# A combination in twelve pieces, single copies of q, and two weight splits two token pairs earlier

## The chip, the cores and the metric

The kernel is one program on one core of a Trainium2 chip. The metric is the device time of one execution in microseconds (us). The engines are TensorE (PE; PEld is its weight load), VectorE (DVE), ScalarE (ACT) and GpSimd (POOL); SyncE (SP) issues most DMAs. Each engine takes its instructions in order.

## The reference

The reference is one decoder layer on 2048 tokens of 1024 columns, in float32. Two mixers read the same normed input; the second is attention over three branches, whose results are weighted with the softmax denominators.

```python
h = rms_norm(x, g_mix[l]); z = h @ w_in[l]
u, gb, gc, q, k, v = jnp.split(z, splits, axis=-1)
y_conv = gb * short_conv(gc * u, conv_w[l])            # causal, depthwise, width 3
q = rms_norm(q, g_q[l]) * HEAD_DIM ** -0.5; k = rms_norm(k, g_k[l])      # 8 heads of 64
y_attn = dilated_mixture(q, k, v)         # (window, dilation) = (128,1), (512,4), (2048,16)
mix = concat(rms_norm(y_conv, g_conv_out[l]), rms_norm(y_attn, g_attn_out[l]))
x = x + mix @ w_out[l]
h = rms_norm(x, g_ffn[l])
x = x + (silu(h @ w_gate[l]) * (h @ w_up[l])) @ w_down[l]
```

## The kernel before

Large products are made of fp16 pairs: a value is a high part and a `low` rest, and three products of such parts replace one in float32. A tile framework orders the instructions of each engine: by the order in which the code writes them, by when a tile's buffer is free, and by `issue_after`, which keeps what stands in its block behind a given instruction.

The stages, in the order of the span:

- **Norms and the first quarter of the conv mixer** (0 to 105 us). `conv_steps` makes channel block `j` in four chunks `c` of 512 tokens. In the first quarter the squares of a chunk (`c2`) are summed over channels by four small TensorE matmuls into a `tr` tile (`squares`, L354, L358); the squares of chunk c − 1 are summed within chunk c, the last ones in `last_squares` (L1211).
- **The q/k/v projection** (105 to 363). Sixteen units `project(g, c)`: group `g` of two heads, token block `c`. The matmuls (L1205) fill banks that ScalarE evacuates (`f`, L1221); then q and k are normed and split (`qkhl`, L1250), stored to DRAM (`d_qk`, L1254) and read back transposed into `qT`, `ka`, `kb` (L199). Beside the units run jobs from a list: `operands` (the next group's weights), `spill_conv` (conv weights through `d_wc`, L1277) and `spill_out` (w_out's raw halves, L1287, split into `t` and stored to `d_wo`, L1306). Raw tiles of w_out and the work tiles of `spill_conv` share the buffers `t4`.
- **Attention** (384 to 712, filled with steps of the conv's other three quarters and of the first part of the output product). 160 units: group, head and branch in the order b = 1, 2, 0, with 8, 4 and 8 units a head. A unit makes scores on TensorE (L1467), exponentials on ScalarE (L1472), the causal band by selects on GpSimd (L1480), a cast on ScalarE (L1483) and `low` on VectorE (L1484). Three units later TensorE makes its output (L1494), and VectorE copies it into `u` (L1499, L1502). Branch 2 reads a copy of q in another token order, `regroup` (L1375, the copies L1380): four copies on VectorE for each head, written at `count` 9 of a group (its second head) and 33 (the next group's first head). `combine` (L1411) adds the three branches' results (L1417, L1418) on GpSimd, takes the reciprocal of the weights' sum with four small VectorE operations (L1420 to L1423), multiplies (L1427) and stores to `d_y` (L1430). It works on eight of sixteen token tiles at once, as four entries of `todo`, due four units on; for the last head it works on four tiles at once on VectorE.
- **The output product** (730 to 905). Eight pairs of token tiles `p` in `out_b`: norm, product, residual, norm for SwiGLU, `hl` stored to `d_h`. Behind two of the pairs stands `left` (L729), the split of a weight's first block for SwiGLU (`w_gate`, then `w_up`): loads `wq`, scaling on ScalarE (L742), sums on GpSimd, rests on VectorE (L723).
- **SwiGLU** (905 to 1720) reads `d_h` transposed; its first products (L812) are evacuated at L863. **The down product** (1720 to 2119) ends the kernel.

Of the kernel before, what the change touches and what calls it, by code (L numbers as in the profile page):

```python
# [18 lines left out]
P = 128  # L19
# [3 lines left out]
NT = S // P  # L23
# [7 lines left out]
class Builder:  # L31
# [170 lines left out]
    def run(self):  # L202
        tc, nc, A = self.tc, self.nc, self.A
        with ExitStack() as ctx:
# [16 lines left out]
            self.dmin = cp.tile([P, 18], F32, name="dmin")  # L221
# [384 lines left out]
    def out_b(self):  # L606
        tc, nc, A = self.tc, self.nc, self.A
        with ExitStack() as c:
# [77 lines left out]
            for p in range(8):  # L686
# [11 lines left out]
                if p in (3, 5):  # L698

                    with tc.issue_after(self.dve.ins), tc.issue_after(self.act.ins), tc.issue_after(self.sp.ins):  # L700
                        self.Wn.append(self.left(A[("w_gate", "w_up")[len(self.Wn)]][0], 0))
# [309 lines left out]
class Fast(Builder):  # L1011
# [22 lines left out]
    def in_and_conv(self):  # L1034
# [5 lines left out]
        with ExitStack() as c:  # L1040
# [42 lines left out]
            n = -1  # L1083
            for step in self.conv_steps(0, W, before):
# [3 lines left out]
                if n == 6:  # L1088
                    norms.close()
                    with tc.issue_after(self.act.ins):  # L1090
                        nc.scalar.preload_act_table_set("natural_log_exp_and_others")
                    self.ring = e(tc.tile_pool(name="ring", bufs=8, side="right"))
# [13 lines left out]
            for n in range(16):  # L1106
# [3 lines left out]
                with ExitStack() as behind:  # L1110
# [13 lines left out]
                    if n == 14:  # L1124
                        self.regroup(self.st0, 0)
# [57 lines left out]
    def project(self, g, c, W):  # L1183
# [27 lines left out]
        def last_squares():  # L1211
            if (g, c) == (0, 0):
                self.squares(3, self.last, self.pstr.tile([P, 4], F32, name="tr"), False)
# [66 lines left out]
    def spill_out(self, half, m):  # L1280
# [4 lines left out]
        for q in range(2):  # L1285
            raw = self.tmp.tile([P, 4, 256], F32, name="t4")
# [22 lines left out]
    def conv_steps(self, j, W, before=None):  # L1309
# [4 lines left out]
        for c in range(4):  # L1314
# [19 lines left out]
            if late is not None:  # L1334
                self.squares(c - 1, late, self.few() if j else self.pstr.tile([P, 4], F32, name="tr"), j > 0)
# [19 lines left out]
            s2 = self.sq[c] if j == 1 else self.cs.tile([P, 512], F32, name="c2", bufs=2)  # L1355
# [5 lines left out]
            late = s2 if j in (0, 3) else None  # L1361
        self.last = late
# [12 lines left out]
    def regroup(self, st, h):  # L1375
# [3 lines left out]
        for n in range(4):  # L1379
            self.nc.vector.tensor_copy(t[:, :, 32 * n:32 * n + 32],  # L1380
                                       st["qT"][:, h, 512 * n:512 * (n + 1)].rearrange("p (a r) -> p r a", r=NT))

# [15 lines left out]
    def attn_steps(self, g, st, nx):  # L1398
# [7 lines left out]
        for h, b in [(h, b) for h in range(2) for b in (1, 2, 0)]:  # L1406
# [4 lines left out]
            def combine(c, n, h=h, last=last):  # L1411

                ts = slice(c, c + n)
                bm = self.at.tile([P, NT], F32, name="bm", bufs=2)[:, 0:n]
                X = [r[:, ts] for r in (U[h, 0], R[h, 1], R[h, 2])]
                e = nc.vector if last else nc.gpsimd
                e.tensor_tensor(X[1], X[1], X[2], op=ALU.add)  # L1417
                e.tensor_tensor(X[0], X[0], X[1], op=ALU.add)  # L1418
                d = 2 * (2 * g + h) + c // n
                nc.vector.tensor_reduce(self.dmin[:, d:d + 1], X[0][:, :, HD], axis=AX.X, op=ALU.min)  # L1420
                nc.vector.tensor_scalar_max(bm, X[0][:, :, HD], 2.0 ** -7)
                nc.vector.reciprocal(bm, bm)
# [472 lines left out]
```

## Time and profile before

| | us |
|---|---|
| median of 3 runs | 2126.46 |
| lowest and highest run | 2121.56, 2128.05 |
| the profiled execution | 2120.59 |
| its span | 2118.8 |
| TensorE busy in it | 2019.1 |
| VectorE, ScalarE, GpSimd busy | 1348.2, 1008.9, 775.3 |

A row of the profile gives the line of the code, the engine, the operation and the tiles (out<-in), a count, and either busy time and mean duration, or a start and a duration; in brackets stands the idle time of the engine ahead of it and what ended that. SPq is SyncE's queue. The granted clock is TensorE's, 1.00 being full speed. Stages are read from the rows' times; one runs into the next.

### The profile page before, as it was taken

The numbers are of one execution on the slowest core, as the hardware profiler recorded it, in microseconds if no ns is written. First come the engines' busy times: TensorE is split into PE (matmuls) and PEld (weight loads), VectorE is DVE, ScalarE is ACT, GpSimd is POOL, SyncE is SP. The second block draws the span as 40 slices with busy tenths as digits, with TensorE's granted clock in tenths as the row PEclk, the third lists the DMA queues.
The fourth block names the chain that finished last, engine by engine and source line by source line (L and its number), as shares of the span: only waits on it lengthen the run. The fifth ranks groups of instructions, "written<-read, shape, count | busy, mean of one in ns | idle before, by whom it ended". The sixth has DMA issues, their size and how long they took to land.

```text
span 2118.8 us, 34786 instructions
## 1 busy us (share of the span) xinstructions
PE 2019.1 (95%) x13368; PEld 1123.8 (53%) x13368; DVE 1348.2 (64%) x2515; ACT 1008.9 (48%) x1780; POOL 775.3 (37%) x809
## 2 busy tenths in 40 slices
PE   4999989999899899989999999999999999999998
PEld 2499989666566544434444444444444444444443
DVE  7455443567777866886767676676768575555453
ACT  7446655666566566552434333334333344343341
POOL 0026535457666521222212212231222245555463
PEclk9999999999999999999999999999999999999999
DMA  9558984356857567995333223322322762431442
GB/s 242 151 136 213 247 205 121 106 151 133 180 139 218 152 191 230 260 296 160 110 109 105 82 92 105 115 87 93 110 100 90 273 238 60 142 117 55 149 140 81
DMA packets 460272, 317.02 MB, mean 150 GB/s; under 512 B 255681, under 2 KB 413377, under 8 KB 457921
## 3 DMA queue, kind: packets, MB, share of 16 engines
q1 hardware_dynamic: 442416, 291.56, 48.4%
q10 hardware_dynamic: 17680, 23.16, 3.0%
q8 instruction: 106, 1.74, 0.3%
q14 instruction: 70, 0.57, 0.1%
HBM read 157.96 MB, written 116.85 MB: 130 GB/s over the span
## 4 chain that ended last, share of the span: by engine, by line
PE 65%; DVE 10%; DMA 8%; ACT 6%; issue 4%; POOL 4%; SPq 3%; DVEq 0%; ACTq 0%; POOLq 0%
PE ps L812 34%; PE ps L945 15%; PE mm L191 3%; PE mm L192 3%; PE mm L193 3%; POOL sm L1480 2%; PE cvx L1205 2%; PE s L1467 1%; PE av L1494 1%; SPq L199 1%; PE mm L1205 1%; DVE vm_a L96 1%; DMA nx_x<-in_x_dram 1%; DVE et L1484 1%; DMA b<-d_h 1%
## 5 line engine op out<-in xcount | busy, mean ns | idle before, releaser
L812 PEld LDWEIGHTS <-w 128*128 128x128 f16 x3696 | 362.2, 98 | 450.7 <-issue 15.3
L812 PE MATMUL ps<-b,w 128*128 128x512 f16 x2112 | 465.4, 381 | 9.9 <-ACT s L863 5.4
L945 PE MATMUL ps<-b,w 128*128 128x512 f16 x1848 | 399.7, 379 | 2.4 <-DVE x L953 1.2
L812 PE MATMUL ps<-hb,w 128*128 128x512 f16 x1584 | 347.1, 379 | 0.8 <-ACT s L863 0.8
L945 PEld LDWEIGHTS <-w 128*128 128x128 f16 x1848 | 180.8, 98 | 221.1 <-issue 3.5
L1205 PEld LDWEIGHTS <-b 128*128 128x128 f16 x3072 | 255.0, 98 | 9.8 <-issue 9.3
L705 POOL TENSOR_TENSOR t<-wq 128x512 f32<-128x512 f32 (+1 forms) x46 | 59.7, 1297 | 407.2 <-issue 230.6
L1480 POOL TENSOR_SCALAR_AFFINE_SELECT sm<-sm 128x256 f32<-128x256 f32 (+2 forms) x288 | 142.2, 517 | 119.9 <-ACT sm L1472 105.8
L818 DVE TENSOR_TENSOR s<-ps,s 128x512 f32<-128x512 f32 x220 | 150.1, 683 | 38.3 <-PE ps L812 37.8
L1484 DVE TENSOR_TENSOR et<-sm,et 128x512 f16<-128x512 f32 (+1 forms) x160 | 129.3, 816 | 67.1 <-ACT et L1483 65.4
L952 POOL TENSOR_TENSOR x<-x,s 128x512 f32<-128x512 f32 x72 | 103.1, 1432 | 171.3 <-DVE s L966 132.2
L1205 PE MATMUL cvx<-w,b 128*128 128x192 f16 x1776 | 151.2, 246 | 0.7 <-ACT f L1221 0.6
L1483 ACT CAST et<-sm 128x512 f16<-128x512 f32 (+1 forms) x160 | 93.8, 589 | 93.3 <-POOL sm L1480 92.3
L953 DVE SCALAR_TENSOR_TENSOR x<-ps,a_u,x 128x512 f32<-128x512 f32 x96 | 71.8, 749 | 101.1 <-PE ps L945 74.3
L1472 ACT ACTIVATE sm<-s,bound,kap 128x512 f32<-128x512 f32 (+1 forms) x160 | 118.6, 747 | 25.9 <-PE s L1467 21.7
L192 PE MATMUL mm<-b,wq 128*128 128x512 f16 x320 | 122.7, 384 | 0.0
L193 PE MATMUL mm<-b,wq 128*128 128x512 f16 x320 | 122.7, 383 | 0.0
L191 PE MATMUL mm<-b,wq 128*128 128x512 f16 x320 | 122.6, 383 | 0.0
L1205 PE MATMUL mm<-w,b 128*128 128x192 f16 x1296 | 113.1, 248 | 8.2 <-ACT f L1221 8.2
L722 ACT CAST w<-t 128x512 f16<-128x512 f32 x88 | 53.7, 616 | 128.6 <-PE ps L812 86.6
L1494 PE MATMUL av<-v,et 128*128 128x65 f16 x1800 | 86.2, 195 | 27.6 <-DVE et L1484 20.4
L96 DVE TENSOR_REDUCE vm_a<-wq 128x1 f32<-128x2048 f32 (+2 forms) x32 | 77.4, 2417 | 41.0 <-DMA wq<-in_w_up_dram 19.8
(289 smaller groups left out, 3242.1 us busy)
## 6 DMA issues: line engine op xcount, KB each, us to landing
d_a<-a ACTq DMA_DIRECT2D x88, 256.0 KB, 2.0
d_wd<-w SPq DMA_DIRECT2D x77, 256.0 KB, 2.0
wq<-d_a SPq DMA_DIRECT2D x64, 256.0 KB, 4.1
b<-d_wd SPq DMA_DIRECT2D x14, 1024.0 KB, 6.6
wq<-in_w_in_dram SPq DMA_DIRECT2D x24, 512.0 KB, 6.5
d_qk<-qkhl SPq DMA_DIRECT2D x16, 768.0 KB, 4.8
d_h<-hl SPq DMA_DIRECT2D x24, 512.0 KB, 3.1
wq<-in_w_gate_dram SPq DMA_DIRECT2D x22, 512.0 KB, 4.7
```

The costliest lines, as they stand in the source:

```text
L191: self.pe = mm(ps, lhsT=lh(k), rhs=rh(k), start=k == ks[0], stop=False)
L192: mm(ps, lhsT=lh(k), rhs=rl(k), start=False, stop=False)
L193: mm(ps, lhsT=ll(k), rhs=rh(k), start=False, stop=k == ks[-1])
L812: nc.tensor.matmul(ps[self.BANK[n]], lhsT=w[:, x, k], rhs=b[:, y, k], start=first and k == 0 and q == 0, stop=k == 3 and q == 2, skip_grou ...
L818: nc.vector.tensor_tensor(t, x, y, op=ALU.add)
L945: nc.tensor.matmul(ps[self.BANK[n]], lhsT=L[n][:, x, f], rhs=B[n][:, f, y], start=first and f == 0 and q == 0, stop=f == n_f - 1 and q == ...
L952: nc.gpsimd.tensor_tensor(o, o, s_, op=ALU.add)
L1205: self.pe = nc.tensor.matmul(ps[:, 192 * t:192 * (t + 1)], lhsT=lh(x, k), rhs=w[:, y, k], start=start and t + k + q == 0, stop=stop and k ...
L1472: nc.scalar.activation(e, sp[:, 0:o], AF.Exp, scale=self.kap, bias=self.bound)
L1480: sel = nc.gpsimd.affine_select(m, m, pattern=pattern, compare_op=ALU.is_ge, fill=0.0, base=0, channel_multiplier=-sg)
L1484: nc.vector.tensor_tensor(et[:, 1], e, et[:, 0], op=ALU.subtract)
L1494: self.pe_av = nc.tensor.matmul(ps[:, us.index(u)], lhsT=p_, rhs=v_, start=n_ == 0, stop=n_ == len(ops) - 1)
```

## The change

Five edits. The four squares of the conv's first quarter are all summed in `last_squares`, in the first unit of the projection, with four `c2` buffers. w_out's raw tiles have a pool of their own (`raws`, two buffers). `regroup` is a generator, and in attention one copy is written at each of the counts 9, 11, 13, 15 and 32, 34, 36, 38, behind that unit's `low`; the block ahead of attention stays whole. `combine` works on four token tiles at once, in twelve steps: add, add with the small operations, and so on four times, then four multiplications with their stores; they are due 2 to 13 units on, one a unit, and `u` has four buffers. The `left` splits stand behind pairs p = 1 and 3 rather than 3 and 5.

```diff
-                if p in (3, 5):
+                if p in (1, 3):
...
+                    self.raws = e(tc.tile_pool(name="raws", bufs=2, side="right"))
...
             if (g, c) == (0, 0):
-                self.squares(3, self.last, self.pstr.tile([P, 4], F32, name="tr"), False)
+                for k in range(4):
+                    self.squares(k, self.sums[k], self.pstr.tile([P, 4], F32, name="tr"), False)
...
-            raw = self.tmp.tile([P, 4, 256], F32, name="t4")
+            raw = self.raws.tile([P, 4, 256], F32, name="raw")
...
-            if late is not None:
-                self.squares(c - 1, late, self.few() if j else self.pstr.tile([P, 4], F32, name="tr"), j > 0)
+            if late is not None and j:
+                self.squares(c - 1, late, self.few(), True)
...
-            def combine(c, n, h=h, last=last):
+            def combine(chunks, e, h=h, last=last):
...
+                for c in chunks:
+                    ts = slice(c, c + 4)
+                    e.tensor_tensor(X[1][:, ts], X[1][:, ts], X[2][:, ts], op=ALU.add)
                     yield
+                    e.tensor_tensor(X[0][:, ts], X[0][:, ts], X[1][:, ts], op=ALU.add)
+                    d, w = 4 * (2 * g + h) + c // 4, X[0][:, ts, HD]
+                    nc.vector.tensor_reduce(self.dmin[:, d:d + 1], w, axis=AX.X, op=ALU.min)
+                    nc.vector.tensor_scalar_max(bm[:, ts], w, 2.0 ** -7)
+                    nc.vector.reciprocal(bm[:, ts], bm[:, ts])
+                    nc.vector.tensor_scalar_mul(bm[:, ts], bm[:, ts], uv)
+                    yield
+                for c in chunks:
+                    ts = slice(c, c + 4)
+                    x = X[0][:, ts, 0:HD]
+                    y = self.y7[:, ts] if last else x
+                    e.tensor_tensor(y, x, bm[:, ts].unsqueeze(2).broadcast_to([P, 4, HD]), op=ALU.mult)
+                    if not last:
+                        i = (2 * g + h) * HD
+                        nc.sync.dma_start(self.d_y.rearrange("(t p) c -> p t c", p=P)[:, ts, i:i + HD], y)
+                    yield
-            Ub = U[h, b] = self.up.tile([P, NT, HD + 1], F32, name="u", bufs=3)
+            Ub = U[h, b] = self.up.tile([P, NT, HD + 1], F32, name="u", bufs=4)
...
-                            for i, step_ in enumerate(c for m in (0, 8) for c in [combine(m, 8)] * 2):
-                                self.todo.append((self.n + 4 + i, lambda step_=step_: next(step_, None)))
+                            steps = combine((0, 4, 8, 12), nc.gpsimd)
+                            for i in range(12):
+                                self.todo.append((self.n + 2 + i, lambda: next(steps)))
...
                     if count == 9:
-                        self.regroup(st, 1)
-                    if count == 33 and g < 3:
-                        self.regroup(nx, 0)
+                        order = self.regroup(st, 1)
+                    if count == 32 and g < 3:
+                        order = self.regroup(nx, 0)
+                    if count in (9, 11, 13, 15, 32, 34, 36, 38):
+                        with self.tc.issue_after(low.ins):
+                            next(order, None)
```

The first place is SyncE's queue in the projection, from the conv weights' stores to the next `d_qk` store. Before, the raws of w_out's first half (`t_1559`, `t_1561`) stand there:

```order
55 L1287 DMA t_1559<-in_w_out_dram 128x4x256
56 L1232 DMA d_v_61<-vs_977 128x4x130
57 L199 DMA_TRANSPOSE ka<-d_qk_132 128x2x512
58 L1277 DMA d_wc_129<-t_1555 128x2048
59 L1135 DMA wq<-in_w_in_dram 128x8x128
60 L1287 DMA t_1561<-in_w_out_dram 128x4x256
61 L1135 DMA wq<-in_w_in_dram 128x8x128 x2
62 L199 DMA_TRANSPOSE kb<-d_qk_132 128x2x512
63 L1254 DMA d_qk_132<-qkhl 128x4x768
```

Now these two raws stand at row 38, ahead of the first of these transposes, and the raws here are those of the next half:

```order
57 L199 DMA_TRANSPOSE ka<-d_qk_132 128x2x512
58 L1280 DMA d_wc_129<-t_1558 128x2048
59 L1137 DMA wq<-in_w_in_dram 128x8x128 x3
60 L199 DMA_TRANSPOSE kb<-d_qk_132 128x2x512
61 L1309 DMA d_wo_81<-t_1815 128x4x256
62 L1309 DMA d_wo_81<-t_1821 128x4x256
63 L1309 DMA d_wo_81<-t_1815 128x4x256
64 L1290 DMA raw<-in_w_out_dram 128x4x256
65 L1235 DMA d_v_61<-vs_963 128x4x130
66 L1309 DMA d_wo_81<-t_1821 128x4x256
67 L1235 DMA d_v_61<-vs_963 128x4x130
68 L1290 DMA raw<-in_w_out_dram 128x4x256
```

The loads from w_out have moved ahead of the group, and the stores of their split (`d_wo`) stand ahead of the next `d_qk`.

The second place is VectorE's queue in attention, at the copies of q for the second head of the second group. Before, the four copies (L1380) stand nearly together, between two of the combination's small operations:

```order
440 L1420 TENSOR_REDUCE dmin<-u 128x1
441 L1421 TENSOR_SCALAR bm<-u 128x8
442 L1380 COPY q_6900<-qT 128x16x32 x3
443 L1422 RECIPROCAL bm<-bm 128x8
444 L1380 COPY q_6900<-qT 128x16x32
445 L1502 COPY u<-av 128x260
446 L1423 TENSOR_SCALAR bm<-bm,uv 128x8
447 L1484 TENSOR_TENSOR et<-sm,et 128x512 x2
```

After, for the same head, the copies (L1385) stand apart; here the second and the third, with `low` (now L1494), copies of outputs (L1512) and conv operations (L1349, L1350) between them:

```order
521 L1385 COPY q_6920<-qT 128x16x32
522 L1430 TENSOR_SCALAR bm<-bm,uv 128x4
523 L1349 SCALAR_TENSOR_TENSOR cg<-cu,convw,cg 128x512
524 L1494 TENSOR_TENSOR et<-sm,et 128x384
525 L1512 COPY u<-av 128x260
526 L1408 TENSOR_SCALAR uv<-uq 128x1
527 L1350 SCALAR_TENSOR_TENSOR cg<-cu,convw,cg 128x512
528 L1494 TENSOR_TENSOR et<-sm,et 128x512
529 L1385 COPY q_6920<-qT 128x16x32
530 L1512 COPY u<-av 128x260
```

Two units lie from one copy to the next.

The third place is GpSimd's queue at a head's combination: the adds (L1417, L1418), the multiplications (L1427) and the selects (L1480) before:

```order
122 L1417 TENSOR_TENSOR r_5617<-r_5617,r_5759 128x520
123 L1480 AFFINE_SELECT sm<-sm 128x2x128 x2
124 L1418 TENSOR_TENSOR u<-u,r_5617 128x520
125 L1480 AFFINE_SELECT sm<-sm 128x512
126 L1417 TENSOR_TENSOR r_5617<-r_5617,r_5759 128x520
127 L1480 AFFINE_SELECT sm<-sm 128x512
128 L1418 TENSOR_TENSOR u<-u,r_5617 128x520
129 L1427 TENSOR_TENSOR u<-u,bm 128x8x64
130 L1480 AFFINE_SELECT sm<-sm 128x512 x2
131 L1427 TENSOR_TENSOR u<-u,bm 128x8x64
```

And the second half of the adds and the first multiplications now (L1423, L1425, L1436, selects L1490):

```order
129 L1425 TENSOR_TENSOR u<-u,r_5619 128x260
130 L1490 AFFINE_SELECT sm<-sm 128x512
131 L1423 TENSOR_TENSOR r_5619<-r_5619,r_5763 128x260
132 L1490 AFFINE_SELECT sm<-sm 128x512
133 L1425 TENSOR_TENSOR u<-u,r_5619 128x260
134 L1490 AFFINE_SELECT sm<-sm 128x2x128
135 L1490 AFFINE_SELECT sm<-sm 128x128
136 L1436 TENSOR_TENSOR u<-u,bm 128x4x64
137 L1490 AFFINE_SELECT sm<-sm 128x2x128 x2
138 L1436 TENSOR_TENSOR u<-u,bm 128x4x64
```

Between two pieces of half as many columns stands one unit's selects.

More of the change, by code (lines that the diff above doesn't have):

```diff
@@ L220, in run @@
             self.eps = cp.tile([P, 3], F32, name="eps")
-            self.dmin = cp.tile([P, 18], F32, name="dmin")
+            self.dmin = cp.tile([P, 32], F32, name="dmin")
             self.low = cp.tile([P, 1], F32, name="low")
@@ L1082, in before @@
                     norm(14, 2)
-            n = -1
+            n, self.sums = -1, []
             for step in self.conv_steps(0, W, before):
@@ L1124, in in_and_conv @@
                     if n == 14:
-                        self.regroup(self.st0, 0)
+                        for _ in self.regroup(self.st0, 0):
+                            pass
                 self.project(g, 3 - i if g == 3 else i, Wg)
@@ L1354, in conv_steps @@
                                     apply_absolute_value=True)
-            s2 = self.sq[c] if j == 1 else self.cs.tile([P, 512], F32, name="c2", bufs=2)
+            s2 = self.sq[c] if j == 1 else self.cs.tile([P, 512], F32, name="c2", bufs=2 if j else 4)
             nc.scalar.activation(s2, y, AF.Square)
@@ L1361, in conv_steps @@
             late = s2 if j in (0, 3) else None
+            if j == 0:
+                self.sums.append(s2)
         self.last = late
@@ L1409, in attn_steps @@
             last = g == 3 and h == 1
-            def combine(c, n, h=h, last=last):
[L1413 to L1422, printed above, removed]
-                nc.vector.tensor_scalar_mul(bm, bm, uv)
-                if not last:
-                    yield
-                y = self.y7[:, ts] if last else X[0][:, :, 0:HD]
-                e.tensor_tensor(y, X[0][:, :, 0:HD], bm.unsqueeze(2).broadcast_to([P, n, HD]), op=ALU.mult)
-                if not last:
-                    i = (2 * g + h) * HD
-                    nc.sync.dma_start(self.d_y.rearrange("(t p) c -> p t c", p=P)[:, ts, i:i + HD], y)
@@ L1431, in attn_steps @@
-            Ub = U[h, b] = self.up.tile([P, NT, HD + 1], F32, name="u", bufs=3)
+            def combine(chunks, e, h=h, last=last):
+                bm = self.at.tile([P, NT], F32, name="bm", bufs=2)
+                X = U[h, 0], R[h, 1], R[h, 2]
+                for c in chunks:
+                    ts = slice(c, c + 4)
+                    e.tensor_tensor(X[1][:, ts], X[1][:, ts], X[2][:, ts], op=ALU.add)
+                    yield
+                    e.tensor_tensor(X[0][:, ts], X[0][:, ts], X[1][:, ts], op=ALU.add)
[13 more added lines that the diff above has]
+                        nc.sync.dma_start(self.d_y.rearrange("(t p) c -> p t c", p=P)[:, ts, i:i + HD], y)
+                    yield
@@ L1483, in attn_steps @@
                     nc.scalar.copy(et[:, 0], e)
-                    nc.vector.tensor_tensor(et[:, 1], e, et[:, 0], op=ALU.subtract)
+                    low = nc.vector.tensor_tensor(et[:, 1], e, et[:, 0], op=ALU.subtract)
                     def output(us=us, pr=pr, et=et, at=at, av=av, b=b, h=h, Vb=Vb, Ub=Ub, step=step, done=pr[-1] == us[-1],
@@ L1503, in output @@
                         if last and b == 0:
-                            for _ in combine(us[0], 4):
+                            for _ in combine(us[0:1], nc.vector):
                                 pass
```

## Prediction

> **What bounds the kernel now.** I read the page first, then TensorE's waits, then tables by stage, and last the rows around each wait that the change touches. The page's first part:
>
> ```profile
> PE 2019.1 (95%) x13368; PEld 1123.8 (53%) x13368; DVE 1348.2 (64%) x2515; ACT 1008.9 (48%) x1780; POOL 775.3 (37%) x809
> ```
>
> TensorE is the bound: of the span of 2118.8 us it idles for 2118.8 − 2019.1 = 99.7 us. A change that leaves its matmuls as they are can win only from these, and from the time in which the clock is held low after them. What TensorE waited for, largest first (total, times, longest):
>
> ```profile
> PE cvx L191 <- DMA b<-ka: 24.8, 1, 24.8
> PE av L1494 <- DVE et L1484: 20.4, 17, 4.2
> PE av L1494 <- DVE u L1502: 5.1, 3, 2.0
> PE av L1494 <- DVE u L1499: 1.2, 1, 1.2
> ```
>
> The 24.8 us are the kernel's first load; the change leaves it. The other three are the attention stage, where most of the change works. Stretches of the span (start and end, width, busy time of PE, PEld, DVE, ACT, POOL with counts, then granted clock, DMA share, GB/s):
>
> ```profile
> 400.00:700.00 300.00, 276.52 (x3178) 186.27 (x3177) 216.77 (x371) 194.06 (x324) 188.75 (x301) 0.98 0.63 157
> ```
>
> ```profile
> 284.00:300.00 16.00, 7.84 (x75) 7.40 (x73) 5.45 (x6) 16.00 (x31) 4.45 (x4) 0.79 0.54 147
> 531.00:540.00 9.00, 5.57 (x40) 3.21 (x41) 6.87 (x11) 2.37 (x4) 4.78 (x7) 0.62 0.69 184
> 905.00:915.00 10.00, 4.57 (x14) 1.67 (x13) 9.96 (x11) 10.00 (x22) 6.33 (x4) 0.66 1.10 325
> ```
>
> In attention TensorE is busy 276.5 of 300 us, so 23.5 us lie idle; VectorE is busy 72% and GpSimd 63%. The three short stretches hold one long wait each (shown below), and the clock is 0.62 to 0.79 there: a wait costs more than itself. After 531, 9.0 × 0.38 = 3.4 us of full clock are missing, part of them inside the wait itself; I charge 2 us to each wait of this size.
>
> **The change part by part.**
>
> *The projection.* The rows of the longest wait, on SyncE's queue, GpSimd, ScalarE and TensorE:
>
> ```profile
> 264.25 8.09 SPq L199 DMA_TRANSPOSE ka<-d_qk  x1
> 277.18 1.90 POOL L1243 TENSOR_TENSOR row<-f,qkr_y 128x1024 f32<-128x1024 f32 x1 [11.58 <-DVE vm_t L101]
> 282.12 0.71 ACT L1250 CAST qkhl<-row 128x256 f16<-128x256 f32 x2 [12.55 <-DMA d_qk<-qkhl]
> 291.96 0.56 ACT L1221 ACTIVATE f<-mm,uq 128x384 f32<-128x384 f32 x1
> 292.57 2.72 PE L1205 MATMUL mm<-w,b 128*128 128x192 f16 x16 [8.16 <-ACT f L1221]
> ```
>
> TensorE has no free bank until ScalarE evacuates at 291.96. ScalarE stood behind its cast at 282.12, held by the store d_qk, which SyncE issues in order behind the raw loads of w_out; those waited for buffers that the split of the conv weights still held. The new pool removes that: SyncE's order after has the raws of the first half ahead of everything in question, those of the second behind the d_wo stores that free them. With a split of w_out one unit ahead of the operands' split, an evacuation stands between the two on ScalarE. Gone is 8.2 and about 1.8 of clock; but the transposes at 264.25 stay and are queued ahead of the same store. Ends: −10 and −4; I take **−8**. Four squares more after conv piece 3 instead of one each:
>
> ```profile
> 78.14 1.05 PE L358 MATMUL tr<-ones,c 128*128 128x1 f32 x8 [1.73 <-ACT c L1356]
> 87.15 0.39 PE L192 MATMUL cvx<-b,wq 128*128 128x512 f16 x1 [2.35 <-DMA b<-kb]
> ```
>
> The work is the same, two groups of eight being moved from ahead of the load wait that ends at 87.15 (where shorter matmul work only lengthens the wait) to behind it, about 1 us each with the edges: **+1.9** (0, if they find another gap, to +2.4). The two more c2 buffers and wider dmin are memory only.
>
> *q's copies.* TensorE's waits beside the last five of the six blocks of four copies that ran in attention:
>
> ```profile
> 449.90 0.22 PE L1494 MATMUL av<-v,et 128*128 128x65 f16 x2 [2.02 <-DVE u L1502]
> 450.64 0.48 PE L1494 MATMUL av<-v,et 128*128 128x65 f16 x10 [0.51 <-DVE et L1484]
> 491.38 0.22 PE L1494 MATMUL av<-v,et 128*128 128x65 f16 x2 [1.53 <-DVE u L1502]
> 492.71 0.48 PE L1494 MATMUL av<-v,et 128*128 128x65 f16 x10 [1.10 <-DVE et L1484]
> 534.43 0.73 PE L1494 MATMUL av<-v,et 128*128 128x65 f16 x10 [4.20 <-DVE et L1484]
> 579.69 0.73 PE L1494 MATMUL av<-v,et 128*128 128x65 f16 x10 [3.63 <-DVE et L1484]
> 624.39 0.22 PE L1494 MATMUL av<-v,et 128*128 128x65 f16 x2 [1.53 <-DVE u L1502]
> 625.72 0.48 PE L1494 MATMUL av<-v,et 128*128 128x65 f16 x10 [1.11 <-DVE et L1484]
> ```
>
> ```profile
> 529.12 3.21 DVE L1380 COPY q<-qT 128x512 f16<-128x512 f16 x3
> L1380 DVE COPY q<-qT 128x512 f16<-128x512 f16 x32 | 23.9, 798 | 0.0
> ```
>
> Their sum is 15.6; ten output matmuls last 0.73 instead of 0.48 after the two longest, where the clock is low: with 2 us for each, 19.6. Four copies (4 × 0.80 = 3.2 us) stood in VectorE's queue ahead of the `low` subtraction that the output waits for. Now one copy follows a `low`, every second unit. A unit lasts 2.05 us (160 from 384 to 712), an output comes three units after its scores, so a delay of 0.8 us is below that slack. But 28 copies stand in attention rather than 24 (one block that had run before it is spread as well), and VectorE, at 72%, must absorb them: 28 × 0.2 = 5.6 stays by my choice. **−14.0**, ends −19.6 and −8. The copies' readers come later than they: the first two of a block are done before unit 40, the others before unit 44. No new wait there.
>
> *The combination.* Its present rows on GpSimd, one there with half as many columns, the selects (column after the bar: busy us, mean ns, idle before), and its small operations on VectorE:
>
> ```profile
> L1418 POOL TENSOR_TENSOR u<-u,r 128x520 f32<-128x520 f32 x14 | 21.6, 1543 | 0.4
> L1417 POOL TENSOR_TENSOR r<-r,r 128x520 f32<-128x520 f32 x14 | 20.8, 1487 | 0.0
> L1427 POOL TENSOR_TENSOR u<-u,bm 128x512 f32<-128x512 f32 x14 | 19.6, 1397 | 10.0 <-DVE bm L1423 7.5 <-DVE cvr_t L52 2.0 <-DVE ssa L362 0.5
> L1253 POOL TENSOR_TENSOR qkhl<-row,qkhl 128x256 f16<-128x256 f32 x32 | 21.8, 703 | 12.3 <-ACT qkhl L1251 12.3
> L1480 POOL TENSOR_SCALAR_AFFINE_SELECT sm<-sm 128x256 f32<-128x256 f32 (+2 forms) x288 | 142.2, 517 | 119.9 <-ACT sm L1472 105.8 <-DVE et L1484 6.9 <-DVE u L1502 3.8
> ```
>
> ```profile
> L1423 DVE TENSOR_SCALAR bm<-bm,uv 128x8 f32<-128x8 f32 (+1 forms) x18 | 7.6, 420 | 0.2
> L1421 DVE TENSOR_SCALAR bm<-u 128x8 f32<-128x8 f32 (+1 forms) x18 | 6.0, 336 | 0.0
> L1422 DVE RECIPROCAL bm<-bm 128x8 f32<-128x8 f32 (+1 forms) x18 | 3.4, 187 | 0.1
> L1420 DVE TENSOR_REDUCE dmin<-u 128x1 f32<-128x8 f32 (+1 forms) x18 | 2.8, 156 | 4.9 <-POOL u L1418 4.9
> ```
>
> GpSimd: 42 operations (62.0 us) become 84. At 256 columns a similar one took 0.70, half of 1.54 is 0.77: 84 × 0.77 = 64.7 us, the same total, but a select behind one waits 0.8 us instead of 3 (two adds together). Attention's waits in the three rows above are 20.4 + 5.1 + 1.2 = 26.7 us; without the copies' 15.6 and the end's 1.2 + 2.3 (below) 7.6 are left. They fall beside these adds and would go. Against it stand 14 more sets of four small VectorE operations, each of (7.6 + 6.0 + 3.4 + 2.8)/18 = 1.10 us: +15.4 us, of which the 28% of free VectorE time covers most; a quarter, 3.9, reaches TensorE. **−3.7**, ends −7.6 and +4. The Trainium skill's page "GPSIMD Engine Reference" (section "Specifications") says that GpSimd's SBUF interfaces are shared with VectorE and contend with VectorE instructions that have two SBUF inputs, as `low` has; the same bytes would then slow it as much in pieces as whole, which makes this term 0 and the sum −22.1. The trace goes further: copies with one input took 3.21/3 = 1.07 us beside GpSimd's work, 0.80 on average. Fourteen more d_y stores go through SyncE, half as large; v and r, queued behind them, are wanted eight units later, so they cost nothing while that lead of 16 us lasts.
>
> *The end of attention.* The last waits, 1.2 and this one, were beside the last combination on GpSimd:
>
> ```profile
> 709.65 0.73 PE L1494 MATMUL av<-v,et 128*128 128x65 f16 x10 [2.33 <-DVE et L1484]
> ```
>
> With clock that is 5 us; the pieces now end later against the tail, so some stays: **−1** (−5 to +3).
>
> *The weight splits of SwiGLU.*
>
> ```profile
> 910.44 1.86 PE L812 MATMUL ps<-b,w 128*128 128x512 f16 x4 [5.43 <-ACT s L863]
> 943.57 2.86 PE L812 MATMUL ps<-b,w 128*128 128x512 f16 x9 [2.71 <-DMA b<-d_h]
> 730.00:830.00 100.00, 97.40 (x460) 44.14 (x460) 69.65 (x168) 61.06 (x120) 21.10 (x26) 0.98 0.73 221
> 830.00:905.00 75.00, 69.30 (x319) 30.89 (x317) 63.42 (x118) 45.08 (x73) 15.36 (x9) 1.00 0.86 252
> ```
>
> The split of the second weight falls at 830 to 905, where VectorE is busy 85%. Two pairs earlier, VectorE has 30 us free in 100; a split costs it some 10 us (63.42 against 0.70 × 75 = 52.2). So it crowds pairs 2 to 4 and frees 5 to 8: the start at 910.44 loses the scaling ahead of its evacuation and should give up 3 of its 5.4, while the later wait at 943.57 rests on transposes through DRAM and grows by about 2 when TensorE comes sooner. **−1** (−6 to +3).
>
> Sum against the profiled execution's 2120.59 us: −8 + 1.9 − 14.0 − 3.7 − 1 − 1 = −25.8. That execution stands 5.9 us below the runs' median of 2126.46, and the difference is carried over: 2126.46 − 25.8 = **2100.7**.
>
> **The rivals.** *A, half comes back.* The projection's wait stays, because the 8.09 us transpose and not the raws holds the store (+8), and the copies each cost their unit 0.35 us instead of 0.2 (+4): −13.8, 2112.7. For it: the transposes' length; against it: the raws are out of that queue in the new order.
>
> *B, the transfers take it back.* All that is won ahead of 905 returns at SwiGLU's start, if that waits on DMA: the share is 1.10 at 905. Then −25.8 becomes about −2: 2124. Against it: only 2.7 us were waited there, and the weights' loads move out of that stretch.
>
> *C, slower: GpSimd's pieces cost by the instruction.* The selects take 142.2/160 = 0.89 us of a unit's 2.05. If a piece of half the columns takes over the other 1.16, the twelve units that hold one overrun. At 1.3: 12 × (1.3 + 0.89 − 2.05) = 1.7 us a head and over seven heads 12, plus the low clock, 2 each, 14, plus 7 × 1.2 as the small operations of VectorE wait behind them: 34 against −25.8, so 2135. Row L1253 speaks against it, since 0.70 us is far below 1.16.
>
> *D, it doesn't do what it says.* The scheduler could pull the pieces or copies together again; the order after does not show it.
>
> **How the numbers follow.** Forecast (−15 to −40) 0.66; A 0.18; B 0.09; C 0.07; D has no time of its own and lies within B. From A almost all is faster by over 0.3% (6.4 us, about what a measurement of this kernel can tell from no change). Range: 2086, where all the better ends but a few come together (−10, 0, −19.6, −7.6, −2, −1: −40), to 2120, which takes in A whole and leaves out B and C. Faster 0.84, same 0.09, slower 0.07.
>
> **What would show it.** Right: no TensorE wait over 2 us between 250 and 300; no [4.20] or [3.63] in attention, and its idle time in that stage from 23.5 to under 10 us; GpSimd's 128x260 adds near 0.77 us; the wait on L863 under 3 us. Wrong: a d_qk store still late behind the transposes (A); the wait of L812 on b<-d_h growing past 10 us (B); 128x260 adds over 1.1 us, and selects as releasers (C).

## The result and the profile after

| | kernel before, us | changed kernel, us | ratio, 95% interval |
|---|---|---|---|
| first comparison, medians | 2127.26 | 2099.47 | 0.9874 (0.9852 to 0.9896) |
| second, beside later experiments | 2121.67 | 2099.82 | 0.9903 (0.9888 to 0.9918) |

The change is worth 27.8 us by the first and 21.8 us by the second; 2100.7 and a gain of 25.8 had been forecast. The changed kernel's median hardly differs; the other one's does. By stage, the profiled executions side with the second. A stage runs here to the end of the last matmul of its kind, or to the start of the next kind (projection L1205, now L1207; outputs of attention L1494, now L1504; SwiGLU L812; down L945):

| stage, us | before | after | after, second profile |
|---|---|---|---|
| up to the projection | 105.0 | 104.0 | 103.3 |
| projection | 265.6 | 260.7 | 259.7 |
| attention | 364.1 | 345.0 | 344.9 |
| output product | 162.5 | 167.5 | 167.0 |
| SwiGLU | 812.9 | 813.9 | 813.1 |
| down product, to the last matmul | 402.0 | 402.3 | 402.4 |

The sum is 2112.1 before, 2093.4 and 2090.4 after: 19 to 22 us. Attention won 19, the first two stages 6 to 8, and the output product gave 4.5 to 5 back. TensorE's row of the page after:

```profile
PE 2017.7 (96%) x13368; PEld 1121.5 (53%) x13368; DVE 1345.2 (64%) x2571; ACT 1009.2 (48%) x1780; POOL 793.9 (38%) x851
```

It idles 2099.9 − 2017.7 = 82.2 us of its span, 17.5 less than before. Its waits, the kernel's first loads left out:

```profile
PE av L1504 <- DVE et L1494: 8.5, 19, 1.2
...
PE ps L812 <- DVE s L818: 4.1, 2, 3.5
PE ps L812 <- DMA b<-d_h: 4.0, 1, 4.0
PE mm L191 <- DVE qT L660: 3.8, 1, 3.8
PE ps L191 <- ACT b L585: 3.0, 1, 3.0
PE av L1504 <- DVE u L1512: 2.5, 2, 1.6
PE ps L812 <- ACT s L863: 2.4, 1, 2.4
...
PE cvx L1207 <- ACT f L1224: 1.9, 2, 1.3
```

The wait on the projection's f is 1.3 at the longest instead of 8.2. In attention no wait on VectorE's `low` (L1494) is over 1.2, where 4.2 and 3.6 stood. What is late next is all behind attention: the output product's waits of 3.0 and 3.8 and SwiGLU's start. The same stretch of attention as before (width, then busy times, clock, DMA share):

```profile
400.00:700.00 300.00, 285.98 (x3295) 192.20 (x3293) 226.74 (x487) 200.84 (x337) 215.64 (x359) 1.00 0.67 167
```

Idle time there is 14.0 us instead of 23.5, and the clock is 1.00 instead of 0.98. The prediction had named under 10 us as a sign of being right; that was missed. The 26.9 us more of GpSimd's work show no cost in this stretch: part is work that stood outside this window before. Its groups, and VectorE's `low` with two of the small operations:

```profile
L1490 POOL TENSOR_SCALAR_AFFINE_SELECT sm<-sm 128x256 f32<-128x256 f32 (+2 forms) x288 | 150.0, 542 | 99.8 <-ACT sm L1482 91.9 <-DVE et L1494 4.2 <-DVE b L586 2.5
L1423 POOL TENSOR_TENSOR r<-r,r 128x260 f32<-128x260 f32 x28 | 25.1, 895 | 0.0
L1425 POOL TENSOR_TENSOR u<-u,r 128x260 f32<-128x260 f32 x28 | 24.6, 878 | 0.0
L1436 POOL TENSOR_TENSOR u<-u,bm 128x256 f32<-128x256 f32 x28 | 20.6, 737 | 0.0
L1494 DVE TENSOR_TENSOR et<-sm,et 128x512 f16<-128x512 f32 (+1 forms) x160 | 117.9, 739 | 68.6 <-ACT et L1493 67.8
L1430 DVE TENSOR_SCALAR bm<-bm,uv 128x4 f32<-128x4 f32 x32 | 13.8, 438 | 0.5
L1428 DVE TENSOR_SCALAR bm<-u 128x4 f32<-128x4 f32 x32 | 10.3, 326 | 0.0
```

The 84 pieces take 70.3 us (62.0 before). Half as many columns cost 895 against 1487 ns, well over half, where 0.77 us had been forecast. A set of small VectorE operations costs with four columns what it did with eight (438 and 326 against 420 and 336 ns).

### The profile page after: what moved, and what is told of

Read it like the earlier page. It is cut to its first block, busy times and chain, and to the rows that moved or that the text cites. A ratio compares the mean times of both kernels' runs of the same rounds, so it can differ in the third digit from the quotient of the medians.

```text
span 2099.9 us, 34888 instructions
## 1 busy us (share of the span) xinstructions
PE 2017.7 (96%) x13368; PEld 1121.5 (53%) x13368; DVE 1345.2 (64%) x2571; ACT 1009.2 (48%) x1780; POOL 793.9 (38%) x851
## 5 line engine op out<-in xcount | busy, mean ns | idle before, releaser
L812 PEld LDWEIGHTS <-w 128*128 128x128 f16 x3696 | 362.5, 98 | 451.4 <-issue 13.3
L812 PE MATMUL ps<-b,w 128*128 128x512 f16 x2112 | 466.1, 382 | 9.9 <-DMA b<-d_h 4.0
L945 PE MATMUL ps<-b,w 128*128 128x512 f16 x1848 | 399.7, 379 | 2.6 <-DVE x L953 1.3
L812 PE MATMUL ps<-hb,w 128*128 128x512 f16 x1584 | 347.2, 379 | 0.6 <-DVE s L818 0.6
L945 PEld LDWEIGHTS <-w 128*128 128x128 f16 x1848 | 180.8, 98 | 221.3 <-issue 3.8
L1207 PEld LDWEIGHTS <-b 128*128 128x128 f16 x3072 | 253.9, 98 | 3.9 <-issue 3.9
L1490 POOL TENSOR_SCALAR_AFFINE_SELECT sm<-sm 128x256 f32<-128x256 f32 (+2 forms) x288 | 150.0, 542 | 99.8 <-ACT sm L1482 91.9
L1494 DVE TENSOR_TENSOR et<-sm,et 128x512 f16<-128x512 f32 (+1 forms) x160 | 117.9, 739 | 68.6 <-ACT et L1493 67.8
L1207 PE MATMUL cvx<-w,b 128*128 128x192 f16 x1776 | 151.6, 246 | 2.5 <-ACT f L1224 1.9
L193 PE MATMUL mm<-b,wq 128*128 128x512 f16 x320 | 121.3, 379 | 0.0
L192 PE MATMUL mm<-b,wq 128*128 128x512 f16 x320 | 121.2, 379 | 0.0
L191 PE MATMUL mm<-b,wq 128*128 128x512 f16 x320 | 121.2, 379 | 0.0
L1207 PE MATMUL mm<-w,b 128*128 128x192 f16 x1296 | 111.5, 246 | 1.0 <-ACT f L1224 0.9
L1504 PE MATMUL av<-v,et 128*128 128x65 f16 x1800 | 86.1, 194 | 14.3 <-DVE et L1494 8.5
```

Of the source, the lines that this page charges most:

```text
L191: self.pe = mm(ps, lhsT=lh(k), rhs=rh(k), start=k == ks[0], stop=False)
L192: mm(ps, lhsT=lh(k), rhs=rl(k), start=False, stop=False)
L193: mm(ps, lhsT=ll(k), rhs=rh(k), start=False, stop=k == ks[-1])
L812: nc.tensor.matmul(ps[self.BANK[n]], lhsT=w[:, x, k], rhs=b[:, y, k], start=first and k == 0 and q == 0, stop=k == 3 and q == 2, skip_grou ...
L945: nc.tensor.matmul(ps[self.BANK[n]], lhsT=L[n][:, x, f], rhs=B[n][:, f, y], start=first and f == 0 and q == 0, stop=f == n_f - 1 and q == ...
L1207: self.pe = nc.tensor.matmul(ps[:, 192 * t:192 * (t + 1)], lhsT=lh(x, k), rhs=w[:, y, k], start=start and t + k + q == 0, stop=stop and k ...
```

## The experiments

My theory was the sum of the prediction: blocks of four copies make most of attention's waits, the combination few, shared buffers the projection's. The rivals were A (the transposes make the projection's wait), and that copies and combination only hurt together or that the combination is the larger part.

### The parts undone one by one

**undo_raws.** The raw tiles share buffers with the conv weights' split again.

```diff
-            raw = self.raws.tile([P, 4, 256], F32, name="raw")
+            raw = self.tmp.tile([P, 4, 256], F32, name="t4")
```

> The changed kernel with one part undone: w_out's raw tiles share the buffers of the conv weights' split again. The changed kernel stands 27.8 us below the kernel before. If the buffers were the cause of the long wait in the projection (the sum's term of -8), this one stands 19 to 21 us below it, and its trace has again one wait of TensorE on ScalarE's f of 6 to 9 us between 250 and 300. If the transposes on SyncE's queue were the cause (rival A), the time stays within 3 us of the changed kernel's, and no such wait is there.

2112.43 us against 2122.84 for the kernel before: 10.4 below it (ratio 0.9952, 0.9938 to 0.9965), where the changed kernel stands 21.8 below. (A distance is always taken from the kernel before as run beside that kernel; the changed kernel itself was run again beside undo_squares, copies_held and six_wide only. The 19 to 21 us expected here had counted from 27.8.) Rows of undo_raws on SyncE's queue, ScalarE and TensorE in the projection:

```profile
264.16 1.02 SPq L1290 DMA_DIRECT2D t<-in_w_out_dram  x1
265.22 8.06 SPq L199 DMA_TRANSPOSE ka<-d_qk  x1
...
276.55 0.53 SPq L1257 DMA_DIRECT2D d_qk<-qkhl  x1
...
281.76 0.71 ACT L1253 CAST qkhl<-row 128x256 f16<-128x256 f32 x2 [10.22 <-DMA d_qk<-qkhl]
...
283.60 3.30 ACT L1305 ACTIVATE t<-t,w_sg 128x256 f32<-128x256 f32 x8 [1.13 <-DVE w_sg L1298]
...
286.80 3.12 ACT L1147 ACTIVATE wq<-wq,w_sg 128x384 f32<-128x384 f32 x6
...
292.83 0.56 ACT L1224 ACTIVATE f<-mm,uq 128x384 f32<-128x384 f32 x1
...
293.44 2.88 PE L1207 MATMUL mm<-w,b 128*128 128x192 f16 x17 [8.53 <-ACT f L1224]
```

The same operations in the changed kernel, from the same transpose on:

```profile
266.05 4.04 SPq L199 DMA_TRANSPOSE ka<-d_qk  x1
...
268.84 3.30 ACT L1305 ACTIVATE raw<-raw,w_sg 128x256 f32<-128x256 f32 x8 [3.57 <-DVE w_sg L1298]
...
282.19 0.56 ACT L1224 ACTIVATE f<-mm,uq 128x384 f32<-128x384 f32 x1
...
282.21 0.61 SPq L1257 DMA_DIRECT2D d_qk<-qkhl  x1
...
285.95 4.16 ACT L1147 ACTIVATE wq<-wq,w_sg 128x384 f32<-128x384 f32 x8 [2.99 <-DVE w_sg L1145]
...
290.02 0.69 ACT L1253 CAST qkhl<-row 128x256 f16<-128x256 f32 x2
...
290.62 0.57 ACT L1224 ACTIVATE f<-cvx,uq 128x384 f32<-128x384 f32 x1
...
291.24 4.12 PE L1207 MATMUL cvx<-w,b 128*128 128x192 f16 x48 [1.34 <-ACT f L1224]
```

The whole wait returns, so the shared buffers are its cause. The path from them to the wait is not the one of the prediction. SyncE does not wait for a buffer there: in undo_raws, as in the kernel before, each of the two raw loads starts about 0.1 us or less after the end of the row ahead. What holds the store is the long transpose behind the second load, 8.06 us instead of 4.04. But the store of the same unit comes no earlier with the change, at 282.21 instead of 276.55, and the cast that needs it landed comes at 290.02 instead of 281.76. The difference is on ScalarE. In undo_raws the scaling of w_out (L1305) and that of the next operands (L1147) both stand behind the late cast and ahead of the evacuation at 292.83, the first since 270.97. In the changed kernel w_out is scaled one unit earlier, with evacuations up to 282.19 behind it, and the operands' scaling is done while ScalarE would otherwise wait for the store; the next evacuation comes 8.4 us after the last. Rival A had the instruction that holds the store, but the wait did not hang on the store alone.

**undo_squares.** Each chunk's squares are summed within the next chunk again.

```diff
-                for k in range(4):
-                    self.squares(k, self.sums[k], self.pstr.tile([P, 4], F32, name="tr"), False)
+                self.squares(3, self.last, self.pstr.tile([P, 4], F32, name="tr"), False)
...
-            if late is not None and j:
-                self.squares(c - 1, late, self.few(), True)
+            if late is not None:
+                self.squares(c - 1, late, self.few() if j else self.pstr.tile([P, 4], F32, name="tr"), j > 0)
```

> The changed kernel with one part undone: each chunk's squares are summed within the next chunk again. By the sum's term of +1.9 it is 2 us faster than the changed kernel. The rival is that the squares find a gap of the conv's first quarter or take one away there (0, or up to 2 us slower); from the traces, the span up to the first matmul of the projection (105.0 before, 104.0 after) should be a little over 1 us longer than with the change, and the projection 2 us shorter.

2100.19 us, beside 2099.82 for the changed kernel; both ratios are 0.9903. The projection begins at 104.2 (103.3 and 104.0 with the change) and takes 258.3 (259.7 and 260.7). Both differences have the expected sign, but kernels that keep the change begin it between 101.7 and 104.0, so the move between the two stages isn't shown, and no cost is seen in the sum.

**undo_copies** and **copies_held.** The four copies stand together again, free to move up in the first, held behind a `low` in the second:

```diff
-                    if count in (9, 11, 13, 15, 32, 34, 36, 38):
-                        with self.tc.issue_after(low.ins):
-                            next(order, None)
+                    if count in (11, 34):                      # copies_held
+                        with self.tc.issue_after(low.ins):
+                            for _ in order:
+                                pass
```

In undo_copies the loop stands at counts 9 and 33, outside `issue_after`.

> The changed kernel with one part undone: q's four copies for a head stand together again, not held behind a low. By the sum's term of -14 it stands 12 to 16 us below the kernel before, with waits of 1 to 4.5 us at each of six blocks. The rival is that the pieces of the combination, not the copies, freed attention: then the blocks no longer meet long GpSimd operations, the waits beside them stay under 1 us each, and the time is within 5 us of the changed kernel's (23 to 28 below the kernel before).

> The changed kernel with q's four copies for a head together, but held behind a low (counts 11 and 34) rather than free to move up. If the spreading wins the copies' 6 us, attention takes 351 us as in undo_copies, with a wait of over 1 us at each block. If it was the place that the scheduler had given the blocks, attention takes 345 to 347 us.

undo_copies took 2109.87 us, 13.0 below the kernel before (0.9932, 0.9919 to 0.9946), its attention 351.1. copies_held took 2101.5, 20.2 below (0.9905, 0.989 to 0.992), its attention 347.4. undo_copies' waits in attention:

```profile
PE av L1504 <- DVE u L1512: 10.3, 7, 2.6
PE av L1504 <- DVE et L1494: 6.3, 13, 0.9
```

and the first of copies_held:

```profile
PE av L1504 <- DVE et L1494: 10.5, 16, 1.9
```

The 13.0 us lie where the term of -14 would have put them, but only because that was counted from a changed kernel at 27.8. Beside its later 21.8, the copies are worth 8.8 us of time; of the attention stage they are worth 6.1. The rival fails too: behind four of the six blocks undo_copies has a wait of 1.3 to 2.6 us, not under 1. Most of the gain comes with holding a block at its place: copies_held is better than undo_copies by 7.2 us in time (the intervals just touch) and by 3.7 in the stage. That spreading the copies adds anything isn't shown. In time copies_held cannot be told from the changed kernel, and the 2.4 us by which its stage is longer are less than two profiles of one kernel can differ (344.6 and 348.0, below).

**undo_pieces.** The combination in four steps of eight token tiles, as in the kernel before (`combine(m, 8)`, two adds before the first yield, due 4 units on), and `dmin` with 18 columns.

```diff
-                            steps = combine((0, 4, 8, 12), nc.gpsimd)
-                            for i in range(12):
-                                self.todo.append((self.n + 2 + i, lambda: next(steps)))
+                            for i, step_ in enumerate(c for m in (0, 8) for c in [combine(m, 8)] * 2):
+                                self.todo.append((self.n + 4 + i, lambda step_=step_: next(step_, None)))
```

> The changed kernel with one part undone: the combination works on eight token tiles at once in four steps again. By the sum's term of -3.7 it stands 24 us below the kernel before, with waits of about 1 us beside the adds of 520 columns. If shared ports make the pieces worth nothing (that term 0) it stands 28 below. If the copies and the combination only hurt where they meet, the copies alone have taken the whole gain: also 28. If the gain of the pieces was under-sized, it stands less than 20 below.

2107.16 us, 15.7 below (0.9923, 0.9909 to 0.9938); attention takes 357.2, with this wait as the largest:

```profile
PE av L1500 <- DVE et L1490: 19.5, 20, 2.8
```

With the spread copies and the old combination the waits on `low` are still 19.5 us in total (20.4 before). So the pieces are worth 12.2 us of the stage, more than three times the 3.7 of the forecast. In time they are worth only 6.1 (15.7 against 21.8, with intervals that overlap), and undo_pieces is even 2.7 us faster than undo_copies, run beside it. Part of that lies behind attention: its output product takes 165.7 us, that of undo_copies 169.4. So the stage says that the pieces win more than the copies; the device time does not show it. In the stage the four combinations add up nearly without a remainder, so the two parts do not hurt only together:

| attention, us | combination as before | in twelve pieces |
|---|---|---|
| copies in blocks | 364.1 | 351.1 |
| copies spread | 357.2 | 345.0 |

**undo_left.** The weight splits behind pairs 3 and 5 again.

```diff
-                if p in (1, 3):
+                if p in (3, 5):
```

> The changed kernel with one part undone: the weight splits stand behind pairs 3 and 5 again. By the sum's term of -1 it stands 27 us below the kernel before. The trace of the changed kernel shows the output product 5.0 us longer than before (167.5 against 162.5 us) and the SwiGLU stage 1.0 longer: if the earlier splits cause that, this kernel is 6 us faster than the changed one, 33 to 35 us below the kernel before.

2104.26 us, 18.6 below the kernel before (0.9913, 0.9898 to 0.9928). It did not come out 6 us faster: the output product takes 166.7, so the longer stage isn't the splits' doing, and SwiGLU takes 817.7, 4 more than with the change, though that stage can differ by 7.5 between two profiles of one kernel (below). Two of its waits there:

```profile
889.02 20.09 PE L812 MATMUL ps<-b,w 128*128 128x512 f16 x84 [5.43 <-ACT s L863]
...
924.04 2.29 PE L812 MATMUL ps<-b,w 128*128 128x512 f16 x5 [4.18 <-DMA b<-d_h]
```

With the change these are:

```profile
897.87 4.44 PE L812 MATMUL ps<-b,w 128*128 128x512 f16 x12 [2.36 <-ACT s L863]
906.34 1.89 PE L812 MATMUL ps<-b,w 128*128 128x512 f16 x4 [4.03 <-DMA b<-d_h]
```

The earlier splits take 3.1 us from the first wait and nothing from the second. In time they win 3.2 us by the distances, but the two intervals overlap (0.9898 to 0.9928 and 0.9888 to 0.9918).

### What of the combination it was

The pieces differ from the old steps in two ways: an operation is half as long, and a unit holds less of them. Two kernels change one at a time.

**dense**: twelve pieces, but in four units as before. **six_wide**: eight token tiles an operation, but one operation every second unit. In six_wide's `combine` a yield stands between the two adds.

```diff
-                                self.todo.append((self.n + 2 + i, lambda: next(steps)))
+                                self.todo.append((self.n + 4 + i // 3, lambda: next(steps)))       # dense
...
+                            lo, hi = combine(0, 8), combine(8, 8)                                   # six_wide
+                            for i, step_ in enumerate((lo, lo, hi, hi, lo, hi)):
+                                self.todo.append((self.n + 2 + 2 * i, lambda step_=step_: next(step_, None)))
```

> The changed kernel with the combination's twelve pieces due in four units of attention instead of twelve, as the eight-wide steps were before. If the wait comes from how much GpSimd work falls into a unit, attention takes 355 us or more again (undo_pieces 357.2), and the kernel loses 8 us or more against the changed one. If the length of a single operation ahead of a select is what counts, attention stays at 345 to 348.

> The changed kernel with the combination in six steps of eight token tiles, one GpSimd operation every second unit, where undo_pieces has two adds of 1.5 us in one unit. If what the pieces win is that two adds no longer follow each other, this stage of attention is within 3 us of the changed kernel's 345.0. If the length of one operation is what counts (1.5 us ahead of a select), it stays near undo_pieces' 357.2, 10 us or more above.

dense took 2106.33 us, 15.6 below the kernel before (0.9925, 0.9909 to 0.9941); attention 353.5, and its waits on `low` are back:

```profile
PE av L1504 <- DVE et L1494: 19.1, 23, 2.5
```

That lies between the two expectations, nearer to the first: of the pieces' 12.2 us, 8.5 are gone when they are crowded. In time dense is 6.2 us behind the changed kernel, with intervals that overlap. six_wide took 2095.03 us (0.9872, 0.9857 to 0.9887), 4.8 below the changed kernel; attention 344.6, with operations of 520 columns again:

```profile
PE av L1501 <- DVE et L1491: 9.0, 16, 1.4
```

```profile
L1425 POOL TENSOR_TENSOR u<-u,r 128x520 f32<-128x520 f32 x14 | 21.6, 1544 | 0.0
L1423 POOL TENSOR_TENSOR r<-r,r 128x520 f32<-128x520 f32 x14 | 18.5, 1324 | 0.0
L1434 POOL TENSOR_TENSOR u<-u,bm 128x512 f32<-128x512 f32 x14 | 16.4, 1175 | 0.0
L1491 DVE TENSOR_TENSOR et<-sm,et 128x512 f16<-128x512 f32 (+1 forms) x160 | 128.0, 806 | 66.1 <-ACT et L1490 64.8
```

So what the pieces won is won by spreading the work over units; cutting the operation in two adds 13.8 us to GpSimd (70.3 against 56.5) and 14 sets of small operations to VectorE, and isn't needed. One thing was not varied alone: undo_pieces and dense begin a head's combination four units on, the two fast kernels two units on.

### A version that beats both

**six_left24** is six_wide run once more, despite its name. **six_left02** and **six_24** are six_wide with the weight splits behind pairs 0 and 2, and 2 and 4 (`if p in (0, 2)`, `if p in (2, 4)`).

> six_wide run again with nothing else changed. It stood 26.6 us below the kernel before (ratio 0.9872), the changed kernel 21.8 in the same call. If that difference is the fourteen fewer sets of small VectorE operations (15.4 us of VectorE, of which the sum let 3.9 through), it is again 3 us or more below the changed kernel's 21.8; if it was chance, it stands about 22 below the kernel before.

> six_wide with the weight splits behind pairs 0 and 2. undo_left showed the splits at 3 and 5 to be 3 us slower than at 1 and 3, the loss standing in SwiGLU's first 100 us. If the loads' distance from the transposes of d_h counts, another pair earlier gives 1 to 3 us more. If VectorE's load in the first pairs counts, the output product takes over 168 us and nothing is won.

> six_wide with the weight splits behind pairs 2 and 4. By the loads' distance it lies between six_wide and the loss of 3 us that splits at 3 and 5 cost: 1 to 2 us slower than six_wide. By VectorE's load it is up to 2 us faster, because the waits at the output product's pair 5 (3.8 to 4.0 us) shrink.

| kernel | median, us | ratio to the kernel before, interval | output product | SwiGLU |
|---|---|---|---|---|
| after_again | 2099.82 | 0.9903 (0.9888 to 0.9918) | 167.0 | 813.1 |
| six_wide | 2095.03 | 0.9872 (0.9857 to 0.9887) | 165.9 | 817.8 |
| the same again | 2093.22 | 0.9862 (0.9841 to 0.9883) | 165.5 | 810.3 |
| six_left02 | 2095.23 | 0.9872 (0.9853 to 0.989) | 170.7 | 808.2 |
| six_24 | 2096.43 | 0.9888 (0.9869 to 0.9906) | 169.2 | 810.4 |

> The changed kernel once more beside the others. By the runs first shown (ratio 0.9874) it stands 27 us below the kernel before; by the two profiled executions, stage by stage, only 19. With undo_raws at 10.4, undo_copies at 13.0 and undo_pieces at 15.7 us below the kernel before, the parts would be worth 16, 14 and 11 us by the one and 9, 6 and 3 by the other; by the stage of attention in the traces the copies are worth 6 and the pieces 12.

The kernel before stood at 2121.67 to 2122.84 us beside the experiments; the changed kernel's 27.8 of the first comparison did not return. six_wide beats the changed kernel by 4.8 us measured side by side, and by 6 to 7 in its second run. Where the splits stand makes no difference in time that can be seen in these three; six_left02 has the longer output product (170.7) that was expected if VectorE's load counts. One stage varies by 3.4 to 7.5 us between two profiles of the same kernel (344.6 and 348.0 in attention, 817.8 and 810.3 in SwiGLU), so single profiles settle no difference of that size.

## Why the prediction was right, and where not

**The projection, −8.** Right in size: 8.5 us of wait returned in undo_raws, and 10.4 against 21.8 in time. Right, too, were the shared buffers as the cause and the step "an evacuation stands between the two on ScalarE". The step "those waited for buffers" was wrong: SyncE waited for none there, and the late store, which the new pool should have freed, stayed late (282.21 against 276.55). My doubt, that the transposes and not the raw loads hold the store, was right about the store and did not matter for the wait.

**The squares, +1.9.** Not seen (0.4 us between the medians, the same ratio). I had counted two groups of work as a pure addition. undo_squares doesn't tell where they were absorbed.

**The copies, −14.0, and the combination, −3.7.** Their sum of 17.7 is near the measured 19.1; the split failed. The step was "Their sum is 15.6": I gave a whole wait to the copies because they stood in VectorE's queue ahead of the late `low`. But the combination's operations of 1.3 to 1.8 us stood on GpSimd close ahead of the same units' selects, and spreading the copies alone left 19.5 us of waits. In the stage the copies are worth 6 to 7 us and the pieces 12 to 13; in time, 8.8 and 6.1. Both put the copies well under 14; how far the pieces stand above 3.7, time does not settle. In the combination's own term, "a select behind one waits 0.8 us instead of 3" put the gain down to halved operations; six_wide has it without halving them, and dense loses most of it with halves, so the spacing counted. The busy time of the added small operations was right: sets of 1.10 us by the forecast, (13.8 + 10.3 + 5.2 + 4.8)/32 = 1.07 measured, with the last two from the same groups:

```profile
L1429 DVE RECIPROCAL bm<-bm 128x4 f32<-128x4 f32 x32 | 5.2, 169 | 0.4
L1427 DVE TENSOR_REDUCE dmin<-u 128x1 f32<-128x4 f32 x32 | 4.8, 151 | 3.7 <-POOL u L1425 3.7
```

The unit of 2.05 us was short for the kernel before: its scores start from 384.6 to 725.8, 2.13 a unit.

The Trainium skill's page "GPSIMD Engine Reference" (section "Specifications") says that GpSimd's SBUF interfaces are shared with VectorE and contended by its instructions with two SBUF inputs. From that I had reasoned that the same bytes slow `low` as much in pieces as whole, and that this term would then be 0. The same bytes did not slow it equally here: `low` took 816 ns before, 806 in six_wide with the same 520 columns, and 739 with pieces of 260. With `low` hardly faster than before, six_wide still won the whole stage, so the time did not hang on this.

**The end of attention, −1.** Wrong by 4 to 6, and the largest miss that no other cancelled. Attention ends 24.8 us sooner (709.8 instead of 734.6), the operand that ScalarE makes for the first pairs (L585, b<-ya,ga) only 22.1 (719.28 instead of 741.40). ScalarE and TensorE in the changed kernel there:

```profile
714.65 0.26 ACT L634 ACTIVATE b<-wq 128x64 f16<-128x64 f32 x1 [4.94 <-POOL wq L631]
...
716.19 0.63 ACT L634 ACTIVATE b<-yb 128x512 f16<-128x512 f32 x1 [1.19 <-DMA yb<-d_y]
```

```profile
719.83 0.39 PE L191 MATMUL ps<-b,b 128*128 128x512 f16 x1 [3.00 <-ACT b L585]
...
721.67 0.63 PE L191 MATMUL mm<-b,b 128*128 128x512 f16 x1
...
838.14 0.58 PE L191 MATMUL mm<-b,b 128*128 128x512 f16 x1 [3.76 <-DVE qT L660]
```

ScalarE's squares for the first pairs wait on GpSimd and a load, and the operand that TensorE wants (L585) stands behind them. The 3.00 us are followed by matmuls of 0.63 us instead of 0.38. The second wait stands behind two reductions of a raw weight tile on VectorE, 4.47 us together:

```profile
832.95 4.47 DVE L96 TENSOR_REDUCE vm_a<-wq 128x1 f32<-128x2048 f32 x2
```

In the kernel before, one such reduction stood there and the wait was half as long; its wait at the first operands was 1.89 us:

```profile
854.39 2.27 DVE L96 TENSOR_REDUCE vm_a<-wq 128x1 f32<-128x2048 f32 x1
```

```profile
732.69 0.39 PE L191 MATMUL mm<-b,b 128*128 128x512 f16 x1 [1.89 <-ACT b L585]
...
858.51 0.38 PE L191 MATMUL mm<-b,b 128*128 128x512 f16 x1 [1.92 <-DVE qT L660]
```

Part of the stage's 4.5 to 5 us is only moved across its border, as that wait of 1.89 lies just ahead of attention's last outputs (734.6): attention and output product together won 14.1 to 14.7 us. What makes the rest in every changed version (165.5 to 170.7 us) wasn't tried.

**The weight splits, −1.** The two waits went as worked out, 5.43 to 2.36 and 2.71 to 4.03. undo_left adds that without the earlier splits the second would have grown as well (4.18), so they win about 3 there; in time that isn't clear of the noise.

**The rivals.** A and D are out; the projection's wait went although the store stayed late. B, the transfers, took back at most a part: the wait on b<-d_h is 4.0, not over 10. C is out as a loss, since a piece takes 0.74 to 0.90 us and not 1.16, but its idea has some truth: the pieces cost more than half, and undoing the cut won 5 us.

That the forecast of 2100.7 was met so closely is in part luck. One error cancelled (copies against pieces). The gain of 25.8 was some 4 us larger than the 21.8 of the second comparison, mostly by what the output product gave back. And the level had 5.9 us added, because the first runs of the kernel before stood that much above its profile; its later medians stand 5 us lower. From the profile alone the sum gives 2094.8, 5 us below the changed kernel.

## What to carry to other kernels

A wait that ends at a late instruction names the queue it stood in, not the work to blame: undo each candidate alone, and in all combinations, before dividing a wait among them. Where a side engine's work disturbs a pipeline, first spread it over more steps at full size; cutting it smaller cost more in all here (70.3 against 56.5 us). A wait that runs through several engines can go although its first link stays late: look also at what stands behind that link in the next engine's queue. Part of what a stage wins can be lost at its end, where the next stage's first operands come less early.

## What the runs showed of the hardware

A DMA transpose that stood for 8.06 us on SyncE's queue directly behind a load of w_out (8.09 in the kernel before) stood for 4.04 and 1.69 in the two profiles of the changed kernel, without that load ahead. In the first of these profiles two other transposes stood for 6.27 and 5.87 us behind loads of w_in. GpSimd's two-input add took 1487 ns for 520 columns and 895 for 260.

TensorE's clock can halve after short waits. In the changed kernel it did after the 3.00 us wait that begins at 716.83: the granted clock was 0.50 from 721.1 to 724.4, and its mean from 715 to 725 is 0.83:

```profile
715.00:725.00 10.00, 7.00 (x26) 2.66 (x25) 6.88 (x23) 6.66 (x16) 1.83 (x5) 0.83 0.27 86
```

The waits of up to 1.2 us on `low` in attention left it at 1.00. The length of a single wait does not decide: in the kernel before, the 1.89 us ahead of 732.69 were followed by 0.50 (733.2 to 736.5), the 2.02 us ahead of 449.90 by 1.00 (448 to 456). The Trainium skill's page "TensorE: Matmul & The Clock Gate" (section "HAM oscillation — how this bites in real kernels") puts the bound at idle gaps over about 3.4 us; here shorter ones were enough.
